# Start addresses of tiles in SBUF: three pads that move the operands of split matmuls to a multiple of 256 bytes

## The chip, the cores and the metric

The kernel runs on one core of a Trainium2 chip. The metric is the device time of one execution in microseconds (us), as the median of the runs. A core has TensorE (PE; its weight loads are listed as PEld), VectorE (DVE), ScalarE (ACT), GpSimd (POOL) and SyncE (SP, whose queue issues most of the DMAs), the memory SBUF with 128 partitions, and the accumulator PSUM.

## What is computed

A sequence of 512 tokens of width 1024 in float32 goes through two blocks of depth 2. Cut to what matters:

```python
# first block, for l in range(2)
mod = silu(c) @ w_ada[l] + b_ada[l]                      # 9 sections of 1024
h = rms_norm(x) * (1 + sc1) + sh1
x = x + 0.5 * g1 * (silu(h @ w_gate) * (h @ w_up)) @ w_ff1_out[l]     # 1024 -> 2816 -> 1024
h = rms_norm(x) * (1 + sc2) + sh2
z = h @ w_in[l]
x = x + g2 * concat(rwkv7(z_a), latent_attention(z_b), retention(z_c)) @ w_out[l]
h = rms_norm(x) * (1 + sc3) + sh3
x = x + 0.5 * g3 * (silu(h @ w_gate) * (h @ w_up)) @ w_ff2_out[l]
# second block, for l in range(2)
u = rms_norm(h) * norm1_g[l]
h = h + concat(pool(u), diff_attention(u), gated_linear_attention(u)) @ w_out_2[l]
h = h + relu(rms_norm(h) @ w_mlp1[l]) ** 2 @ w_mlp2[l]                # 1024 -> 4096 -> 1024
```

## The kernel before

Everything is kept with the features on the partitions and the 512 tokens along a row of 2048 bytes. A float32 product is made of three matmuls: each operand is split into a high and a low part of the type float32r, and `gemm_k` (line 405) issues high x high, high x low and low x high into one PSUM tile. `weight` (line 381) loads a block of weights, up to 1024 columns, into a `raw` tile by one DMA of the SP queue, ScalarE copies its 512-column halves into the high tile and VectorE subtracts to get the low tile; both are `wr` tiles. The activations are split in the same way by `split` (line 440) and `modulate`, into tiles of the classes `r` and `h`.

In a matmul's name in the profile, `ps<-a,b`, `a` is the operand that streams through (moving) and `b` the one that is loaded as weights (stationary). All large products are of this kind: `ps<-ff_h,wr` (feed-forward, in), `ps<-ff_r,wr` (feed-forward, out), `ps<-mix_h_x,wr`, `ps<-mix_r,wr`, `ps<-wr,mix_r` (the mixers' projections; the last has the weights moving), `ps<-mix_r_x,wr` and `ps<-mix_r_y,wr` (out of the first mixer), `ps<-mlp_r,wr` (both MLP products). Other matmuls of the mixers are plain float32; each of these shows as two records.

The program runs through the phases feed-forward, mixer 1, feed-forward, twice, then mixer 2, MLP, twice. The order of the instructions is fixed when the program is built. A dry pass notes the first and the last use of each tile, and `Alloc.assign` (line 175) gives each one of the fixed buffers of its class, by program order alone; sizes of tiles play no part in it. Each instruction is issued by `Spy` at line 136, so the profile shows L136 for all.

Where a tile lies follows from the order in which pools are opened and from the tiles' sizes, each rounded up to 32 bytes. `setup` (line 338) opens the constants: `ident`, `vec`, `masks`, `rows`, `ones`, then `x` (8 tiles of 2048 bytes), `mods`, `ident_r`. Then come the classes of `GLOBAL` (line 210) in their order: `raw`, `wr`, `m`, `mr`, `sq` (`ps` is PSUM). Behind them each phase opens its own classes (`KIND`, line 219; `PHASES`), and mixer 1 has places that pass from one class to another (`STAGES`, line 227): `va`, `big`, `s`, `r`, `h`. In the program of the kernel before, the first constant starts at byte 16,512 of a partition. The start of each tile, as its remainder by 256 bytes (its residue):

| tiles | start of the first, bytes | residue |
|---|---|---|
| `x` | 20,480 | 0 |
| `ident_r` | 37,824 | 192 |
| `raw` | 38,336 | 192 |
| `wr` | 50,624 | 192 |
| `m` | 75,200 | 192 |
| `mr` | 78,784 | 192, 224, 0, 32 |
| `sq` | 78,912 | 64 |
| all 512-column tiles of the phases (`s`, `r`, `h`) and `big`, `rw` | 80,960 | 64 |
| the same in the third stage of mixer 1 behind `va` (`mix_s_w`, `mix_r_y`, `mix_r_x`) | 193,728 for the last `mix_r_y` | 192 |

A slice of 128 columns of a weight tile starts at a multiple of 512 bytes from the tile's start, and half the tokens at 1024 bytes, so a slice has its tile's residue. The top of the allocation is at byte 228,544.

Of the kernel before, what the change touches and what calls it, by code (L numbers as in the profile page):

```python
# [12 lines left out]
F32 = mybir.dt.float32  # L13
F32R = mybir.dt.float32r
# [4 lines left out]
PSUM = bass.MemoryType.PSUM  # L19

P = 128
# [26 lines left out]
# ---------------------------------------------------------------- host layout  # L48
def blocks(w, cols=P):
    """[K, N] -> [N/cols, 128, K/128*cols]: one contiguous run per partition and block."""  # L50
    k, n = w.shape
    return np.ascontiguousarray(
        w.reshape(k // P, P, n // cols, cols).transpose(2, 1, 0, 3)
    ).reshape(n // cols, P, (k // P) * cols)


def group_blocks(w, groups):
    """[K, N] -> per group of K chunks: [N/128, 128, kg*128], flattened and joined."""
    return np.concatenate([blocks(w[a * P:(a + n) * P]).ravel() for a, n in groups])
# [11 lines left out]
OUT2_ROWS = np.r_[0:256, 768:1024, 256:768]  # L71
TWO_PI = (6.28125, 0.0019350051879882812, 3.019916e-07)


def make_masks():
    """constants that depend on shapes alone."""
# [23 lines left out]
def make_rows():  # L100
    """rotary frequencies and the sign of the sine, per partition, for head widths 64 and 32."""
    out = np.zeros((P, 4), np.float32)
    base = np.float32(10000.0)
    for j, d in ((0, 64), (2, 32)):
        inv = base ** (-np.arange(0, d, 2, dtype=np.float32) / np.float32(d))
        out[:, j] = np.tile(inv, P // (d // 2))
        out[:, j + 1] = np.where(np.arange(P) % d < d // 2, -1.0, 1.0)
    return out
# [11 lines left out]
# ---------------------------------------------------------------- device side  # L120
# [4 lines left out]
class Spy:  # L125
    """an engine that notes which tiles each instruction names, then issues it."""
# [21 lines left out]
class Alloc:  # L148
    """Tiles by class. A dry pass notes where each is used first and last in program order; from that each gets
    one of the class's fixed buffers, so that the buffers never force an order that the program doesn't have."""  # L150
# [17 lines left out]
    def begin(self, cls, key, n):  # L168
        """buffers (key, 0..n-1) that serve the class until `end`."""
# [5 lines left out]
    def assign(self, sizes):  # L175
        """key of the buffer for every tile, in the order of their birth."""
# [6 lines left out]
    def assign_with(self, sizes, keep):  # L183
        """the same, with `keep` buffers of a class held back from what fits into one that comes and goes."""
# [25 lines left out]
# class of buffer -> (shape, type, count); the phase's own classes follow  # L210
# [4 lines left out]
    "mr": ([P, 8], F32R, 4),  # L215
# [3 lines left out]
KIND = {"s": ([P, S], F32), "r": ([P, S], F32R), "h": ([P, S], F32R), "big": ([P, 1024], F32), "rw": ([P, 2048], F32), "va": ([P, 516], F32)}  # L219
# [6 lines left out]
# places of the first mixer that change their use: the stages' classes; "x" lies where "h" of the phase "ff" does  # L226
# [7 lines left out]
class Build:  # L234
# [36 lines left out]
    def stage(self, i):  # L271
        """the places from the first that changes on pass over to the classes of stage i."""
# [31 lines left out]
    def lend_x(self):  # L304
        """put x into DRAM; until it is back its tiles serve as the phase's slots."""
# [32 lines left out]
    def setup(self):  # L338
        nc, c = self.nc, self.const
        self.ident = c.tile([P, P], F32, name="ident")  # L340
# [14 lines left out]
    def background(self, share=None):  # L355
        """part of the work that goes on behind the first block's wide products (share None: all that is left)."""
# [23 lines left out]
    # -- weights: one block, split exactly into two float32r parts  # L380
    def weight(self, ap, n, cls="wr", sub=None):
        """(hi, lo) tiles of 512 columns each."""
# [17 lines left out]
    def gemm(self, out, w, x, ks, m=P, at=0, sl=ALL):  # L400
        """out[m, 512] = sum_k w_k^T x_k, each product of split parts; w's chunks from column `at` on."""
# [3 lines left out]
    def gemm_k(self, out, w, xk, i, n, m=P, at=0, sl=ALL):  # L405
        """chunk i of n of such a product."""
# [7 lines left out]
    def out_proj(self, load, g, update, norm=None, scale=None):  # L414
        """x[j] from its products with g, for all j. norm "sum": with the sums of squares of the next norm, the last
        j's left to `pending`; "halves": with the norm itself, the last two j by halves of the tokens, so that the first half's is there early."""
# [33 lines left out]
    # -- rsqrt of a small positive tile by DVE  # L450
# [14 lines left out]
    def sum_sq(self, acc, xc, sl=ALL):  # L465
        """acc + xc^2 (acc None: a new sum)."""
# [10 lines left out]
    def x_done(self, j, sl=ALL):  # L477
        """chunk j of x has its final value of this stage: its part of the next norm."""
        self.xsq = self.sum_sq(None if j == 0 else self.xsq, self.x[j], sl)

    def norm_half(self, i):
        """PSUM [128, 512], half i of the tokens: one over the norm of x."""
# [3 lines left out]
    def rms_col(self, chunks, dim, eps, ts=range(4)):  # L486
        """[128, 4]: 1/sqrt(mean over features of x^2 + eps) of token ts[t]*128 + partition; chunks None: of x."""
# [15 lines left out]
    def bcast(self, r, ts=range(4)):  # L503
        """PSUM [128, 512] with the token's value on every partition."""
# [9 lines left out]
    # -- adaptive layer norm: one section of 1024 columns  # L514
    def cond_row(self):
        """silu(c) on every partition."""
# [13 lines left out]
    def ada_dot(self, l, s, k, w):  # L530
        """chunk k of section s of 1024 columns of the modulation of layer l, less its bias."""
# [3 lines left out]
    def ada_end(self, l, s, k=0, n=KD):  # L535
        """chunks k.. of section s with their bias, and what is derived from them."""
# [10 lines left out]
    def ada_steps(self, parts):  # L547
        """the sections (layer, section) one after the other in small steps, loads ahead of them."""
# [13 lines left out]
    def modulate(self, i, k, hk, pr, sl=ALL, pool=True):  # L562
        """chunk k of h = rms_norm(x) * (1 + sc) + sh, split into hk."""
# [13 lines left out]
    def modulated(self, i, ws):  # L577
        """h of modulation i, a list of (hi, lo), and its products with the first weights, by halves of the tokens
        and as the chunks come."""
# [11 lines left out]
    def start(self):  # L591
        """the first h: its modulation is worked out chunk by chunk as the weights for it come in."""
# [26 lines left out]
    def ff(self, l, w, i, norm):  # L619
        """x += 0.5 * g * (silu(h w_gate) * (h w_up)) w_out"""  # L620
# [32 lines left out]
    # ------------------------------------------------------------ constants  # L653
    def restart(self):
        """factors of a scan over the tokens that starts anew with every chunk of 64."""
# [9 lines left out]
    def rotary_tables(self):  # L665
        """cos and signed sin of positions * inv, [128, 512] each, for head widths 64 and 32."""
# [26 lines left out]
    def derived(self, l):  # L693
        """small per-feature vectors worked out on chip for layer l of the first block."""
# [14 lines left out]
    # ------------------------------------------------------------ first mixer: RWKV-7  # L709
# [11 lines left out]
    def rwkv_z(self, l, h, ps, dv, z):  # L721
        """nine projected tiles after the centred shift (r 0-1, k 2-3, v 4-5, gate, decay and rate inputs);
        v with the chunks of each pair swapped."""
# [16 lines left out]
    def head_bcast(self, col, stride, at):  # L740
        """PSUM [128, 512] from token-major scalars of two heads, col[tok, t*stride + at + hh]."""
# [10 lines left out]
    def head_sums(self, src, dst, at):  # L752
        """dst[tok, t*2 + at + hh] = sum over the head's 64 features of src [features, tok]."""
# [4 lines left out]
    def rwkv_norm(self, l, z, j):  # L758
        """one over the norm of each head's keys, token major."""
# [19 lines left out]
    def rwkv_prep(self, l, z, dv, lora, j):  # L779
        """the four scaled operands of each direction for one pair of heads.  # L780

        pr: [d, step pair, (p | r), (par, t)]; qm: [d, step pair, par, (q | m swapped by par), t]
        """
# [57 lines left out]
    def rwkv_inverse(self, os_):  # L841
        """X^T of every chunk, X = (1 + strict part)^-1: per pair of heads and direction
        [128 (par, s)][(step pair, hh), t]."""
# [29 lines left out]
        # matrix (j, m, d, (par, half)) on its own partition, m = (step pair, hh)  # L873
# [37 lines left out]
    def rwkv_blocks(self, xt, xa, u):  # L911
        """from the inverses of the 32 x 32 diagonal blocks those of the chunks, for one pair of heads."""
        nc = self.nc
        # off-diagonal 32-blocks
# [34 lines left out]
    def rwkv_pair(self, o, vs, xt, xd, ip):  # L949
        """per-chunk matrices of one pair of chunks in each direction: what the sequential steps need.  # L950
        xd: zeros, and room for the inverses of both chunks on the diagonal."""
# [88 lines left out]
    def rwkv_heads(self, l, z, o, xt, gate, j, out):  # L1040
        """one pair of heads: sequential steps over the chunks, head norm, bonus, gate."""
# [5 lines left out]
        # the state by turns in two halves, both heads' [key, value] on the diagonal for each direction  # L1047
# [32 lines left out]
        # head norm (the values were centred, so the mean is zero), gain, bonus, gate  # L1080
# [54 lines left out]
    # ------------------------------------------------------------ first mixer: latent attention  # L1135
# [19 lines left out]
    def rope32(self, out, pz, n, tab):  # L1155
        """rotary over 32-wide heads on n partitions; pz in PSUM."""
# [8 lines left out]
    def mla_norms(self, l, z):  # L1165
        """the two latent norms, in place."""
# [8 lines left out]
    def mla_first(self, z, i, pk, pq, kq, qpe):  # L1175
        """operands of head i: [64 plain, 32 rotary, 1 for the maximum] x tokens, split."""
# [9 lines left out]
        # the maximum of a row of scores, taken of the rounded operands: any number near it serves  # L1186
        mx, mr = self.small_t(4, "mla_max"), self.get("mr")
# [10 lines left out]
    def mla_second(self, i, kq, va, ot):  # L1198
        """softmax and values of head i, keys on partitions; ot[tok, (tile, hh, v)]."""
# [29 lines left out]
    def mla_pair(self, ot):  # L1229
        """the values of a pair of heads, features on partitions, split."""  # L1230
# [12 lines left out]
    def mla(self, l, z, out, others):  # L1243
# [4 lines left out]
        # rotary part of the queries, four heads a tile  # L1248
# [9 lines left out]
        # values, token major, a column of ones between the two heads of a pair  # L1258
# [728 lines left out]
```

## Time and profile before

| | |
|---|---|
| time, median of 3 runs | 3662.97 us (3648.62, 3662.97, 3664.79) |
| span of the profiled execution (its own time isn't listed apart) | 3653.2 us |
| TensorE busy | 3528.1 us (97%), 17786 matmuls |
| VectorE busy | 2103.8 us (58%) |
| ScalarE busy | 1436.7 us (39%) |
| GpSimd busy | 281.7 us (8%) |
| DMA moved | 375.78 MB, 103 GB/s on average |

The span is the time from the first to the last instruction of one profiled execution; the device time has a little more around it. Busy times overlap between engines. Matmuls are pipelined: the end of one is modelled, the next starts before it, and so a mean duration of 395 ns doesn't say how far apart two matmuls are. How far apart they are is read from the start times in the timeline. [...] Residues stand in no view; they come from the table above.

### The profile page before, as it was taken

The numbers are of one execution on the slowest core, as the hardware profiler recorded it, in microseconds if no ns is written. First come the engines' busy times: TensorE is split into PE (matmuls) and PEld (weight loads), VectorE is DVE, ScalarE is ACT, GpSimd is POOL, SyncE is SP. The second block draws the span as 40 slices with busy tenths as digits, with TensorE's granted clock in tenths as the row PEclk, the third lists the DMA queues.
The fourth block names the chain that finished last, engine by engine and source line by source line (L and its number), as shares of the span: only waits on it lengthen the run. The fifth ranks groups of instructions, "written<-read, shape, count | busy, mean of one in ns | idle before, by whom it ended". The sixth has DMA issues, their size and how long they took to land. (4 is left out here: it accounts for less than half of the span.)

```text
span 3653.2 us, 46456 instructions
## 1 busy us (share of the span) xinstructions
PE 3528.1 (97%) x17786; PEld 2849.3 (78%) x17786; DVE 2103.8 (58%) x4153; ACT 1436.7 (39%) x2644; POOL 281.7 (8%) x344
## 2 busy tenths in 40 slices
PE   7999998999999999999899999999999999999998
PEld 5888876788888888887678888877778887778887
DVE  7954785657954534468565544366754445764444
ACT  3223544444233423245344423245443334443333
POOL 2000261100000000015210000000100000000000
PEclk9999998999999999999898999999999999999999
DMA  7833322015842222332201222221122222212222
GB/s 273 323 123 103 120 81 54 24 46 207 322 164 95 86 97 87 96 121 81 61 18 41 76 93 94 96 83 64 54 94 93 97 94 72 65 58 98 93 93 75
DMA packets 132879, 375.78 MB, mean 103 GB/s; under 512 B 37712, under 2 KB 41072, under 8 KB 132656
## 3 DMA queue, kind: packets, MB, share of 16 engines
q1 hardware_dynamic: 127808, 359.48, 29.7%
q0 software_dynamic: 3776, 12.32, 1.0%
q8 instruction: 139, 2.28, 0.3%
q10 hardware_dynamic: 1072, 1.01, 0.1%
q14 instruction: 84, 0.69, 0.1%
HBM read 362.27 MB, written 10.49 MB: 102 GB/s over the span
## 5 line engine op out<-in xcount | busy, mean ns | idle before, releaser
L136 ACT CAST wr<-raw 128x512 fp32r<-128x512 f32 (+2 forms) x1054 | 640.8, 610 | 1558.7 <-PE ps L136 1438.5
L136 DVE TENSOR_TENSOR wr<-raw,wr 128x512 fp32r<-128x512 f32 (+1 forms) x1004 | 681.4, 680 | 782.3 <-ACT wr L136 760.6
L136 PE MATMUL ps<-ff_h,wr 128*128 128x512 f32 (+1 forms) x4296 | 983.7, 390 | 10.1 <-ACT ff_h L136 7.3
L136 PEld LDWEIGHTS ps<-ff_h,wr 128*128 128x128 f32 x4296 | 794.4, 190 | 195.4 <-ACT ff_h L136 10.1
L136 PE MATMUL ps<-mlp_r,wr 128*128 128x512 f32 (+1 forms) x3120 | 716.3, 391 | 2.1 <-ACT mlp_r L136 2.1
L136 PEld LDWEIGHTS ps<-mlp_r,wr 128*128 128x128 f32 x3120 | 580.9, 188 | 135.7 <-ACT mlp_r L136 3.0
L136 PE MATMUL ps<-ff_r,wr 128*128 128x512 f32 (+1 forms) x2238 | 495.2, 382 | 0.0
L136 PEld LDWEIGHTS ps<-ff_r,wr 128*128 128x128 f32 x2238 | 404.1, 188 | 89.3
L136 PE MATMUL ps<-mix_r,wr 128*128 128x512 f32 (+1 forms) x1104 | 277.9, 402 | 1.8 <-DVE mix_s L136 1.8
L136 PE MATMUL ps<-mix_h_x,wr 128*128 128x512 f32 (+2 forms) x1104 | 261.0, 395 | 4.3 <-ACT mix_h_x L136 2.2
L136 PEld LDWEIGHTS ps<-mix_r,wr 128*128 128x128 f32 (+1 forms) x1104 | 199.4, 185 | 57.9 <-issue 5.2
L136 PEld LDWEIGHTS ps<-mix_h_x,wr 128*128 128x128 f32 (+1 forms) x1104 | 200.4, 197 | 56.0 <-issue 4.5
L136 DVE SCALAR_TENSOR_TENSOR ff_big<-ff_big,ff_big 128x1024 f32<-128x1024 f32 x144 | 176.5, 1238 | 10.3 <-DMA ff_big<-in_w_ada 9.6
L136 DVE SCALAR_TENSOR_TENSOR ff_s<-ff_s,ps 128x512 f32<-128x512 f32 x176 | 120.2, 684 | 88.1 <-PE ps L136 83.7
L136 DVE SCALAR_TENSOR_TENSOR x<-ps,hg,x 128x512 f32<-128x512 f32 (+1 forms) x102 | 73.4, 719 | 85.9 <-PE ps L136 85.7
L136 DVE TENSOR_TENSOR ps<-ps,mlp_s 128x512 f32<-128x512 f32 (+1 forms) x66 | 45.1, 683 | 105.3 <-PE ps L136 105.2
L136 ACT COPY mix_s<-ps 128x256 f32<-128x256 f32 (+7 forms) x156 | 61.6, 401 | 104.4 <-PE ps L136 75.8
L136 DVE TENSOR_TENSOR mlp_r<-mlp_s,mlp_r 128x512 fp32r<-128x512 f32 x80 | 54.6, 691 | 69.5 <-ACT mlp_r L136 69.5
L136 POOL MEMSET mix_s<- 32x256 f32 (+3 forms) x36 | 12.5, 348 | 985.6 <-DVE mix_r L136 363.9
L136 ACT ACTIVATE mix_s<-ps,m 128x512 f32<-128x512 f32 (+3 forms) x140 | 70.9, 529 | 44.0 <-PE ps L136 25.0
L136 PE MATMUL ps<-mix_s,mix_s 128*128 128x128 f32 (+7 forms) x648 | 82.7, 283 | 2.6 <-ACT mix_s L136 1.9
L136 PEld LDWEIGHTS ps<-mix_s,mix_s 128*128 128x128 f32 (+5 forms) x648 | 63.6, 169 | 16.9 <-ACT mix_s L136 7.1
(317 smaller groups left out, 3591.8 us busy)
## 6 DMA issues: line engine op xcount, KB each, us to landing
raw<-in_ff_in SPq DMA_DIRECT2D x176, 512.0 KB, 3.5
ff_big<-in_w_ada SPq DMA_DIRECT2D x144, 512.0 KB, 6.2
raw<-in_mlp SPq DMA_DIRECT2D x128, 512.0 KB, 3.5
raw<-in_ff_out SPq DMA_DIRECT2D x64, 448.0 KB, 3.3
raw<-in_ff_out SPq DMA_DIRECT2D x32, 512.0 KB, 3.6
raw<-in_out SPq DMA_DIRECT2D x32, 512.0 KB, 3.5
raw<-in_in SPq DMA_DIRECT2D x28, 512.0 KB, 3.5
raw<-in_in_a SPq DMA_DIRECT2D x18, 512.0 KB, 4.0
```

The lines of the kernel that those rows point to most:

```text
L136: self.alloc.last[self.name] = f(*a, **k)
```

## The change

Three pads and nothing else that reaches the program (comments and docstrings are taken out too): one constant tile of 16 floats (64 bytes) ahead of all others; `mr` gets 32 columns instead of 8 (128 bytes instead of 32, four tiles); `va` gets 528 columns instead of 516 (2112 bytes instead of 2080 after rounding, four tiles). The two uses of the padded tiles take a slice of the old width. By adding up, `raw`, `wr`, `m`, `mr`, `sq`, `ident_r` and all tiles of the phases then start at residue 0 (`va` at 0, 64, 128 and 192), `x` at 64, and the top of the allocation is at byte 229,120.

```diff
+LINE = 256
+ALIGN_PAD = 16
...
-    "mr": ([P, 8], F32R, 4),
+    "mr": ([P, 32], F32R, 4),
...
-KIND = {"s": ([P, S], F32), "r": ([P, S], F32R), "h": ([P, S], F32R), "big": ([P, 1024], F32), "rw": ([P, 2048], F32), "va": ([P, 516], F32)}
+KIND = {"s": ([P, S], F32), "r": ([P, S], F32R), "h": ([P, S], F32R), "big": ([P, 1024], F32), "rw": ([P, 2048], F32), "va": ([P, 528], F32)}
...
     def setup(self):
         nc, c = self.nc, self.const
+
+        c.tile([P, ALIGN_PAD], F32, name="align_pad")
         self.ident = c.tile([P, P], F32, name="ident")
...
-        mx, mr = self.small_t(4, "mla_max"), self.get("mr")
+        mx, mr = self.small_t(4, "mla_max"), self.get("mr")[:, :8]
...
             v = self.get("va")
-            v3 = v.rearrange("p (n b) -> p n b", n=4)
+            v3 = v[:, :516].rearrange("p (n b) -> p n b", n=4)
```

## Rows read from the trace of the kernel before

**Rows 1.** Page, busy time, share of the span and instructions of each engine:
```profile
PE 3528.1 (97%) x17786; PEld 2849.3 (78%) x17786; DVE 2103.8 (58%) x4153; ACT 1436.7 (39%) x2644; POOL 281.7 (8%) x344
```

**Rows 2.** TensorE's waits: for whom, us in total, times, longest; first and last of 16:
```profile
PE ps L136 <- DVE sq L136: 27.1, 7, 17.2
...
PE ps L136 <- POOL ff_h L136: 0.4, 2, 0.2
```

**Rows 3.** Stretches: us, busy of PE, PEld, DVE, ACT, POOL; clock, DMA share, GB/s:
```profile
90.00:120.00 30.00, 30.00 (x130) 24.31 (x129) 29.76 (x55) 9.28 (x16) 0.00 (x0) 1.00 0.93 328
2740.00:2923.00 183.00, 183.00 (x789) 148.39 (x788) 77.10 (x116) 69.00 (x114) 0.00 (x0) 1.00 0.29 95
```

**Rows 4.** Groups of TensorE by shape, whole span: count, busy us, mean ns, idle before:
```profile
L136 PE MATMUL ps<-ff_h,wr 128*128 128x512 f32 x4008 | 942.2, 396 | 5.9 <-ACT ff_h L136 5.5 <-DVE ff_h L136 0.3
L136 PE MATMUL ps<-mlp_r,wr 128*128 128x512 f32 x3024 | 704.3, 395 | 2.1 <-ACT mlp_r L136 2.1
L136 PE MATMUL ps<-ff_r,wr 128*128 128x512 f32 x1986 | 464.4, 395 | 0.0
L136 PE MATMUL ps<-mix_r,wr 128*128 128x512 f32 x1056 | 265.8, 403 | 0.0
L136 PE MATMUL ps<-mix_h_x,wr 128*128 128x512 f32 x864 | 220.8, 413 | 1.7 <-DVE mix_s L136 1.7
...
L136 PE MATMUL ps<-wr,mix_r 128*128 128x512 f32 x192 | 46.2, 398 | 2.9 <-ACT mix_r L136 2.9
```

**Rows 5.** Timeline of TensorE, dense stretches: start us, length us, run, count:
```profile
2699.74 60.58 PE L136 MATMUL ps<-mlp_r,wr 128*128 128x512 f32 x260
...
2200.86 59.43 PE L136 MATMUL ps<-ff_h,wr 128*128 128x512 f32 x254
```

**Rows 6.** Timeline of TensorE, end of mixer 1, first and last of five blocks:
```profile
2021.27 2.20 PE L136 MATMUL ps<-mix_r_y,wr 128*128 128x512 f32 x9
...
2043.03 2.20 PE L136 MATMUL ps<-mix_r_y,wr 128*128 128x512 f32 x9
```

**Rows 7.** Timeline of TensorE, first feed-forward stage, weights in `ff_r` tiles:
```profile
63.57 1.98 PE L136 MATMUL ps<-ff_h,ff_r 128*128 128x512 f32 x8
```

**Rows 8.** Timeline of TensorE, two runs of 24 with `wr` moving:
```profile
2446.09 5.83 PE L136 MATMUL ps<-wr,mix_r 128*128 128x512 f32 x24
...
1880.67 5.71 PE L136 MATMUL ps<-wr,mix_r_x 128*128 128x512 f32 x24
```

**Rows 9.** By tile, durations min/median/max ns: 2700 to 2760 us, 2021 to 2047 us:
```profile
L136 PE MATMUL ps<-mlp_r,wr x260: 390/393/404, 2699.7 to 2759.9; 128*128 128x512 f32 x130
...
L136 PE MATMUL ps<-mix_r_x,wr x71: 389/389/389, 2020.8 to 2046.9; 128*128 128x512 f32 x71
```

**Rows 10.** Timeline of 256-column runs; below, plain float32 groups (count, busy, mean ns):
```profile
526.83 9.40 PE L136 MATMUL ps<-wr,mix_h_x 128*128 128x256 f32 x77 [0.68 <-DVE wr L136]
...
2049.22 1.96 PE L136 MATMUL ps<-mix_r_x,wr 128*128 128x256 f32 x15
...
L136 PE MATMUL ps<-x,x 64*128 64x512 f32 x32 | 15.8, 615 | 0.0
L136 PE MATMUL ps<-mix_s_x,mix_s 128*64 128x512 f32 x28 | 10.8, 618 | 0.0
```

**Rows 11.** Groups of TensorE by shape, first 183 us:
```profile
L136 PE MATMUL ps<-ff_h,wr 128*128 128x512 f32 x369 | 92.3, 408 | 5.6 <-ACT ff_h L136 5.2 <-DVE ff_h L136 0.3
L136 PE MATMUL ps<-ff_r,wr 128*128 128x512 f32 x192 | 44.8, 394 | 0.0
```

**Rows 12.** Groups of VectorE by shape, whole span, the subtraction that makes a low part:
```profile
L136 DVE TENSOR_TENSOR wr<-raw,wr 128x512 fp32r<-128x512 f32 x926 | 641.7, 694 | 728.9 <-ACT wr L136 720.3 <-PE ps L136 6.8
L136 DVE TENSOR_TENSOR mlp_r<-mlp_s,mlp_r 128x512 fp32r<-128x512 f32 x80 | 54.6, 691 | 69.5 <-ACT mlp_r L136 69.5
```

## The prediction

> **What bounds the kernel now.** I read the page's busy times first: TensorE is busy in 3528.1 us, 97% of the span [rows 1]. The list of TensorE's waits comes next: its longest entry, over the whole span, is 27.1 us and its last 0.4 [rows 2], so there is little waiting to remove. [...] So the question is the step from one matmul's start to the next one's, and whether it depends on where the operands lie.
>
> The busy column can't answer that (matmuls overlap); the timeline can, because a run of n equal matmuls lasts n-1 steps plus the duration of the last. In the dense runs of the change's main operands, 260 matmuls take 60.58 us and 254 take 59.43 us [rows 5]; less a last duration of 0.39 us these are 60.19 / 259 = 232.4 ns and 59.04 / 253 = 233.4 ns a step. In both, the moving operand (`mlp_r`, `ff_h`) starts at residue 64 of 256 bytes and the stationary one (`wr`) at residue 192.
>
> The kernel before also holds pairs at *equal* residues, and these are my experiment. In the last projection of the first mixer, both `mix_r_x`/`mix_r_y` and `wr` are at 192. There the blocks of nine that begin at 2021.27 and 2043.03 us [rows 6] are 4 x 24 matmuls apart: 21.76 us / 96 = 226.67 ns. All durations in that stretch are 389 ns, where the dense MLP run spreads over 390 to 404 with a median of 393 [rows 9]; the modelled duration moves one for one with the step. A second pair has both operands at 64: eight matmuls of `ff_h` with `ff_r` in 1.98 us [rows 7], (1.98 - 0.39) / 7 = 227 ns. The control is moving `wr` (192): with stationary `mix_r` at 64, 24 matmuls take 5.83 us; with stationary `mix_r_x` at 192, 5.71 us [rows 8]. Both runs follow small matmuls and contain their own start, so their means, 5.44 / 23 = 236.5 and 5.32 / 23 = 231.3 ns, stand a little above the settled steps; the difference is 5.2 ns a step. So neither 64 nor 192 is bad in itself: unlike residues cost about 6 ns a matmul, in either direction.
>
> **What the change does, part by part.** No instruction is added or removed and no order changes; the dry pass sees the same uses, so each tile gets the same buffer number. Only addresses move. I add them up from the sizes: the 64-byte pad takes `raw`, `wr` and `m` from residue 192 to 0; the wider `mr` (4 x 96 bytes more) takes the phase pools `s`, `r`, `h`, `big`, `rw` from 64 to 0; the wider `va` (4 x 32 bytes more) takes the third-stage pools `mix_r_y`, `mix_r_x` from 192 to 0. The top of the allocation goes from 228,544 to 229,120 bytes of a partition. After it, moving and stationary operands of the split products start at the same residue, 0; `x` goes the other way, from 0 to 64.
>
> *Large matmuls.* The 512-column products with unlike residues are six groups: 4008 + 1986 + 3024 + 1056 + 864 + 192 = 11,130 [rows 4]. I take the step to fall to 226.67 ns wherever TensorE is the bound.
> - Feed-forward stages: 4008 + 1986 less the 369 + 192 of the first 183 us [rows 11] leave 5433. The measured steps of such stretches lie between 232.4 and 233.4, so 5.7 to 6.7 ns, mean 6.2: 33.7 us.
> - MLP stages: 3024 x 5.7 ns = 17.2 us.
> - Mixer stages: 1056 + 864 + 192 = 2112, x 5.8 ns = 12.2 us if all were dense; mean durations of 403 and 413 against 395 [rows 4] show waits among them, and a wait swallows the gain before it. I keep three quarters, 9.2 us; the ends are 5 and 12.
> - First 183 us: 561 x 5.8 = 3.2 us at most. But VectorE is busy 29.76 of 30 us there, at a DMA share of 0.93 [rows 3], so a faster TensorE meets the modulation's dot products. I keep 0.5; the ends are 0 and 3.2.
> - Start after a wait: the like run of rows 8 is 5.32 - 23 x 0.2267 = 0.11 us above the settled step, the unlike one 5.44 - 23 x 0.2324 = 0.09. So a start costs the like pairs some 0.02 us more; the list of waits has 16 entries with 73 waits [rows 2], 1.5 us. I take off 2.
>
> The sum is 33.7 + 17.2 + 9.2 + 0.5 - 2 = 58.6 us.
>
> *Half-width matmuls* (256 columns): a run at 192/64 has 77 in 9.40 us, 9.12 / 76 = 120.0 ns; one at 192/192 has 15 in 1.96 us, 1.68 / 14 = 120.0 ns [rows 10]. I count 0.
>
> *Plain float32 matmuls* (not split): 512 columns with both operands at 0 take 615 ns, with both at 64 618 ns [rows 10]. No trend that I could use, so 0; the bound is 3 ns on some 4080 records, 12 us either way, and most of these stand beside waits of the mixers.
>
> *VectorE, ScalarE, DMA.* The same subtraction takes 694 ns on tiles at 192 and 691 on tiles at 64 [rows 12]: 0, and it is hidden in dense stretches anyway (77 of 183 us busy). If that cover went, 3 ns on 926 subtractions would be 2.8 us. The weight transfers are at 0.29 of the DMA engines there [rows 3]; a TensorE that is 2.5% faster asks for 0.30. No wait changes and nothing is queued behind anything new.
>
> [...] Rows 8 show the step of one moving operand change with the place of the stationary one alone. [...]
>
> **The rivals.**
> 1. *Nothing moves* (3663 us). The like pairs of the kernel before might be fast for something else that they share, such as the stretch they stand in, or residue 0 might not behave like 64 and 192. For: no split product in the trace has both operands at 0, and the longest like stretch (rows 6) is some 30 us. Against: two places, three operand pairs, and the control in both directions. This is also "the change doesn't do what it says". Chance 0.11.
> 2. *It settles on the slow step* (slower). Moving and stationary operands, and the tiles being written, now all start at residue 0; if two streams that start alike at 0 got into each other's way at every matmul, each one would pay what only some pay now. The place is the dense stretch and the price is the slowest matmul of it: 404 ns, 15 above 389 [rows 9], so a step of 226.7 + 15 = 241.7 instead of 232.9 (the mean of the two runs of rows 5), 8.8 ns x 11,130 = 98 us: 3761 us. It decides the sign as soon as the mean step at 0/0 is above 232.9 ns. Against it: the like pairs at 64 and at 192 do the opposite. Chance 0.04.
> 3. *The fast step doesn't hold*: with raw tiles, weights and every pool at one residue, writes of ScalarE, VectorE and the DMAs start where the reads do and throw TensorE out of the fast step again and again. Half of the gain: 3663 - 29 = 3634 us. Against: in the stretch of rows 6 VectorE and ScalarE write `wr` at 192 as well, and all durations stay at 389. Chance 0.06.
> 4. *More than that*: residue 0 is better still. [...] Nothing in the trace points to it. Chance 0.03.
>
> **How the numbers follow.** The forecast has 0.76. The profiled execution has a span of 3653.2 us; its own time isn't listed beside the three runs (3648.62 to 3664.79, median 3662.97), so I take the 9.8 us between span and median as what lies around it and leave it alone. The span becomes 3653.2 - 58.6 = 3594.6 us, the median 3604 us (-1.6%). Its own bounds: at best 36.4 (5433 x 6.7 ns) + 17.2 + 12.2 + 3.2 = 69 us, from the lowest of the runs 3580; at worst 31.0 (5433 x 5.7 ns) + 17.2 + 5 - 2, less the 12 us of the float32 matmuls, 39 us, from the highest run 3626. To hold 8 in 10 the range reaches on to rival 3: 3580 to 3640. About 0.5% (18 us) is what a measurement of this kernel can tell from no change. Faster by more than that: forecast, rivals 3 and 4, 0.85; within it: rival 1, 0.11; slower: rival 2, 0.04.
>
> **What would show it.** In the profile after, a dense run of `mlp_r` with `wr` must have a step of 226.67 ns, so 260 matmuls in 59.1 us instead of 60.58, with a median duration of 389. The three feed-forward groups must fall alike, the 256-column runs and the subtractions must not move. If dense durations stay at 393, rival 1 holds; at 400 or more, rival 2; if they jump between 389 and 393 or more within a run, rival 3. The forecast is wrong by size if the steps are right but the mixers or the first 183 us give back more than the 6 us I left out: then TensorE's waits grow by that amount.

## The result, and the profile after

The changed kernel takes 3600.8 us (median of four runs, 3596.28 to 3616.28), the kernel before, beside it on the same chip, 3658.47 us (four runs, 3648.62 to 3664.79). The ratio is 0.9854 with a 95% interval of 0.9826 to 0.9881: 57.7 us less, faster by three times the 0.5% that a measurement of this kernel can tell. The forecast was 3604 us and 58.6 us less.

The page of the kernel after, its span and its busy times (us, share, instructions):

```profile
span 3614.5 us, 46456 instructions
PE 3487.3 (96%) x17786; PEld 2858.0 (79%) x17786; DVE 2100.4 (58%) x4153; ACT 1437.4 (40%) x2644; POOL 281.3 (8%) x344
```

The work is the same, instruction for instruction, and only TensorE's time is less [rows 1]. This profiled execution is the slowest of the four, 3616.28 us; a later run of the same kernel has a span of 3597.9 us. Why its span fell by only 38.7 us is told below, with the first mixer.

The groups by shape answer [rows 4] (count, busy us, mean ns, idle before):

```profile
L138 PE MATMUL ps<-ff_h,wr 128*128 128x512 f32 x4008 | 918.0, 390 | 5.7 <-ACT ff_h L138 5.3 <-DVE ff_h L138 0.3
L138 PE MATMUL ps<-mlp_r,wr 128*128 128x512 f32 x3024 | 687.4, 389 | 2.1 <-ACT mlp_r L138 2.1
L138 PE MATMUL ps<-ff_r,wr 128*128 128x512 f32 x1986 | 452.1, 389 | 0.0
L138 PE MATMUL ps<-mix_r,wr 128*128 128x512 f32 x1056 | 261.4, 399 | 0.0
L138 PE MATMUL ps<-mix_h_x,wr 128*128 128x512 f32 x864 | 215.5, 407 | 2.1 <-DVE mix_s L138 2.1
L138 PE MATMUL ps<-wr,mix_r 128*128 128x512 f32 x192 | 46.9, 403 | 2.9 <-ACT mix_r L138 2.9
```

Line 138 here is line 136 of before. Read the busy column against [rows 4]: -24.2, -16.9, -12.3, -4.4, -5.3, +0.7, together -62.4 us over 11,130 matmuls. The mean of the MLP group is now the smallest duration, 389: nearly all of its matmuls run at the same pace.

The timeline of dense stretches (start us, length us, run, count) answers [rows 5]:

```profile
2199.70 60.68 PE L138 MATMUL ps<-ff_h,wr 128*128 128x512 f32 x267
2699.74 60.46 PE L138 MATMUL ps<-mlp_r,wr 128*128 128x512 f32 x266
```

(60.46 - 0.39) / 265 = 226.7 ns, and (60.68 - 0.39) / 266 = 226.7 ns, where [rows 5] gave 232.4 and 233.4. Durations by tile, minimum, median and maximum in ns, from 2700 to 2760 us, to be read against the first line of [rows 9]:

```profile
L138 PE MATMUL ps<-mlp_r,wr x266: 389/389/389, 2699.7 to 2759.8; 128*128 128x512 f32 x133
```

The stretches answer [rows 3] (us, busy of PE, PEld, DVE, ACT, POOL, granted clock, DMA share, GB/s):

```profile
90.00:120.00 30.00, 30.00 (x134) 24.86 (x133) 30.00 (x55) 10.21 (x17) 0.00 (x0) 1.00 0.91 338
2740.00:2923.00 183.00, 183.00 (x809) 151.56 (x808) 78.96 (x119) 69.78 (x116) 0.64 (x2) 1.00 0.28 96
```

In the dense stretch 809 matmuls start where 789 did, 2.5% more, at the same granted clock of 1.00: the gain is not a higher clock.

From the first matmul of a phase to the first of the next (the last MLP to the end of the span), in us, read from the timelines of four profiled executions:

| | feed-forward, four stages | MLP, two | second mixer, two | first mixer, two |
|---|---|---|---|---|
| before | 1514.9 | 736.0 | 479.9 | 895.6 |
| before, once more | 1516.5 | 737.3 | 482.7 | 882.2 |
| after | 1478.4 | 719.2 | 477.7 | 912.2 |
| after, once more | 1478.4 | 719.2 | 474.6 | 899.0 |

As an example, the lines between which the first MLP lies, of the kernel before (361.06 us):

```profile
2676.74 8.20 PE L136 MATMUL ps<-mlp_r,wr 128*128 128x512 f32 x34 [1.04 <-ACT mlp_r L136]
...
3037.80 8.41 PE L136 MATMUL ps<-wr,mix_r 128*128 128x512 f32 x35 [1.88 <-ACT mix_r L136]
```

and of the kernel after (352.56 us):

```profile
2656.81 8.11 PE L138 MATMUL ps<-mlp_r,wr 128*128 128x512 f32 x34 [1.06 <-ACT mlp_r L138]
...
3009.37 9.84 PE L138 MATMUL ps<-wr,mix_r 128*128 128x512 f32 x35 [1.88 <-ACT mix_r L138]
```

The feed-forward stages give 36.5 us, the MLP stages 16.8, the second mixer 2.2 to 5.3 (first row against the last two). The first mixer gives nothing that can be seen: its length varies by more than its gain from one execution of the same program to the next.

### The profile page after: what moved, and what is told of

Read it like the earlier page. It is cut to its first block, busy times and chain, and to the rows that moved or that the text cites. A ratio compares the mean times of both kernels' runs of the same rounds, so it can differ in the third digit from the quotient of the medians.

```text
span 3614.5 us, 46456 instructions
## 1 busy us (share of the span) xinstructions
PE 3487.3 (96%) x17786; PEld 2858.0 (79%) x17786; DVE 2100.4 (58%) x4153; ACT 1437.4 (40%) x2644; POOL 281.3 (8%) x344
## 5 line engine op out<-in xcount | busy, mean ns | idle before, releaser
L138 PE MATMUL ps<-ff_h,wr 128*128 128x512 f32 (+1 forms) x4296 | 960.7, 385 | 9.5 <-ACT ff_h L138 7.1
L138 PE MATMUL ps<-mlp_r,wr 128*128 128x512 f32 (+1 forms) x3120 | 699.4, 386 | 2.1 <-ACT mlp_r L138 2.1
L138 PE MATMUL ps<-ff_r,wr 128*128 128x512 f32 (+1 forms) x2238 | 483.0, 377 | 0.0
L138 PE MATMUL ps<-ident,mix_s 128*128 128x128 f32 x384 | 59.4, 299 | 20.5 <-DVE mix_s L138 20.2
```

Of the source, the lines that this page charges most:

```text
L138: self.alloc.last[self.name] = f(*a, **k)
```

## The experiments

The theory: what sets the step of a 512-column split matmul is whether its moving and its stationary operand start at the *same* residue by 256 bytes; the value of the residue does not matter, nor does the place of `raw`. The rivals: it is the multiple of 256 itself that is fast, for the moving operand, for the weights, or for the raw tiles that ScalarE and VectorE read; or only some distances between the operands are slow. Later, three forms of the theory had to be told apart. Where an expectation speaks of 1a, 1b and 1c: in 1a the matmul pays whose own operands are unlike, in 1b the one that runs while unlike weights are loaded, and in 1c an unlike operand takes the fast step away from a whole stretch.

All edits are to the changed kernel. A pad class takes room in a partition and is used by nothing. Ratios go by the runs of the kernel before on the same chip.

| run | residue of weights / moving | time, us (n: one run) | ratio, 95% interval | step, dense stages, ns |
|---|---|---|---|---|
| `like_at_64` | 64 / 64 | 3593.72 | 0.9848 [0.9795, 0.9901] | 226.7 |
| `like_at_32` | 32 / 32 | 3594.71 | 0.9855 [0.981, 0.9901] | 226.7 |
| `first_pad_alone` | 0 / 128 | 3662.48 | 1.0016 [0.9984, 1.0047] | 232.9, 233.3 |
| `apart_by_phase` | 0 / 32 to 224 | 3661.37 (n) | | 228.9 to 234.3 |
| `after_beside` | 0 / 0 | 3603.92 | 0.9866 [0.9826, 0.9905] | 226.7 |
| `raw_apart` | 0 / 0, `raw` at 128 | 3603.79 | 0.9852 [0.982, 0.9883] | 226.7 |
| `low_weights_apart` | high parts 0, low parts 128 / 0 | 3645.72 (n) | | 231.1 |
| `odd_tiles_apart` | 0 / 0 and 128 by turns, first MLP | 3627.36 (n) | | 232.5 there |
| `third_stage_apart` | 0 / 128 in one stage | 3618.12 (n) | | 232.4 there |

**Like residues elsewhere (`like_at_64`, `like_at_32`).** The first pad is 128 (or 96) bytes instead of 64. `mr` goes back to its old width, and a pad of 128 bytes behind it keeps the phases at the residue of the weights.

```diff
-ALIGN_PAD = 16
+ALIGN_PAD = 32
...
-    "mr": ([P, 32], F32R, 4),
+    "mr": ([P, 8], F32R, 4),
+    "pad_b": ([P, 32], F32, 1),
```

For `like_at_32` the first constant is 24.

> Weights, raw tiles and the phases' pools all start at residue 64 of 256 bytes instead of 0 (the pad ahead of the constants is 128 bytes, 128 bytes stand behind mr). Theory 1, equal residues: as fast as the changed kernel, ratio to before 0.985, dense step 226.67 ns, all durations 389. Theory 2, the multiple of 256 itself: as before, ratio 1.00, step 232 to 233 ns, durations 390 to 404.

> The same with residue 32, so that no operand starts at a multiple of 64 bytes. Theory 1, equal residues: ratio 0.985, step 226.67 ns. Theory 2, the multiple itself (256, 128 or 64): ratio 1.00 or above, step 232 ns or more.

Durations by tile from 2700 to 2760 us, of the kernel at 64:

```profile
L138 PE MATMUL ps<-mlp_r,wr x267: 389/389/390, 2699.7 to 2759.9; 128*128 128x512 f32 x134
```

and of the kernel at 32:

```profile
L138 PE MATMUL ps<-mlp_r,wr x267: 389/389/390, 2699.6 to 2759.9; 128*128 128x512 f32 x134
```

Neither kernel has a weight tile or a 512-column tile at a multiple of 256, and both have the whole gain, with ratios that can't be told from that of the change. The multiple of 256 that the change aims at is not what works; that the operands are alike is. Nor is it the remainder by 512: in the kernel at 64, by adding up, `wr` starts at byte 50,752 (64 more than a multiple of 512) and the first `r` tile of the MLP at 105,792 (320 more), and the gain is whole. By its ratio no kernel tried here beats the changed one; these two equal it.

**The first pad alone (`first_pad_alone`).** `mr` and `va` go back to their old widths. `raw` and `wr` stay at 0, the phases go to 128.

```diff
-    "mr": ([P, 32], F32R, 4),
+    "mr": ([P, 8], F32R, 4),
...
-KIND = {"s": ([P, S], F32), "r": ([P, S], F32R), "h": ([P, S], F32R), "big": ([P, 1024], F32), "rw": ([P, 2048], F32), "va": ([P, 528], F32)}
+KIND = {"s": ([P, S], F32), "r": ([P, S], F32R), "h": ([P, S], F32R), "big": ([P, 1024], F32), "rw": ([P, 2048], F32), "va": ([P, 516], F32)}
```

> Only the first of the three pads: raw and weight tiles at residue 0, the pools at 128, so unlike by 128 as in the kernel before (64 and 192) but with the weights at a multiple of 256. Theory 1, equal residues: no gain, ratio 1.00, step 232 to 233 ns. Theory 2 in the form that the weights' place alone counts: ratio 0.985, step 226.67 ns.

```profile
L138 PE MATMUL ps<-mlp_r,wr x258: 392/396/398, 2719.8 to 2779.8; 128*128 128x512 f32 x129
...
L138 PE MATMUL ps<-mix_r_x,wr x67: 389/389/390, 2023.7 to 2046.8; 128*128 128x512 f32 x67
```

Aligned weights and raw tiles alone are worth nothing: 1.0016. In the same kernel the last stage of the first mixer, where moving tiles happen to lie at 0 like the weights, runs at 389. So the fast and the slow step stand side by side in one execution, and the place tells them apart.

**All distances (`apart_by_phase`).** A class opened first in six of the phases moves their tiles by 32 to 224 bytes; the weights stay at 0.

```diff
+APART = {0: 96, 2: 32, 3: 64, 5: 160, 7: 192, 9: 224}
...
+            apart = APART.get(self.nphase, 0)
...
-            classes = {c: (*KIND[c], n) for c, n in PHASES[name].items()}
+            classes = {"gap": ([P, apart // 4], F32, 1)} if apart else {}
+            classes.update({c: (*KIND[c], n) for c, n in PHASES[name].items()})
```

> Weights at 0 and each phase's pools at a distance of its own: feed-forward stages 96, 32, 64 and 160 bytes, MLPs 192 and 224, mixers 0. One look at the steps of each phase. Theory 1, equal residues: every phase but the mixers is back at 232 to 233 ns, some 15 us a feed-forward stage counting 1500 matmuls at 6 ns is 9 us, all six 54 us, so about 3655 us. A finer rule (distances that are multiples of 64 are alike, say): 64 and 192 stay at 226.67 ns and 32, 96, 160, 224 don't.

(The expectation's 15 us for a stage is a slip: 1500 matmuls at 6 ns are 9 us.) The timeline, one run from each stage, in the order 96, 32, 64, 160, 192, 224:

```profile
248.98 39.36 PE L138 MATMUL ps<-ff_r,wr 128*128 128x512 f32 x168
...
1004.73 55.46 PE L138 MATMUL ps<-ff_h,wr 128*128 128x512 f32 x237
...
1299.75 36.32 PE L138 MATMUL ps<-ff_h,wr 128*128 128x512 f32 x158
...
2208.79 51.47 PE L138 MATMUL ps<-ff_h,wr 128*128 128x512 f32 x219
...
2719.62 60.59 PE L138 MATMUL ps<-mlp_r,wr 128*128 128x512 f32 x259
...
3329.73 60.60 PE L138 MATMUL ps<-mlp_r,wr 128*128 128x512 f32 x259
```

Length less 0.39, by the count less one: 233.3, 233.3, 228.9, 234.3, 233.3 and 233.4 ns. With the 232.4 to 233.4 at a distance of 128, six of the seven unlike distances cost the same 6 to 8 ns. The seventh, the moving tile 64 bytes on from the weights, costs 2.2; 64 bytes the other way (192) costs the full price. So it is not a matter of distance alone, and no run shows why 64 stands out.

**The raw tiles (`raw_apart`).** Weights and phases at 0 as in the change; `raw` goes to 128 and `x` to 192.

```diff
-ALIGN_PAD = 16
+ALIGN_PAD = 48
...
+    "pad_c": ([P, 32], F32, 1),
...
-    "mr": ([P, 32], F32R, 4),
+    "mr": ([P, 8], F32R, 4),
+    "pad_b": ([P, 32], F32, 1),
```

`pad_c` stands between `raw` and `wr`.

> Weights and pools at residue 0 as in the changed kernel, but the raw tiles at 128 and x at 192. Theory 1, only the two operands of a matmul count: ratio 0.985, dense step 226.67 ns, the subtraction into wr near 694 ns, the weight transfers near 3.5 us to landing. Theory 2, the place of the raw form has a part in the gain (the DMA that writes it, or the copy that reads it): ratio between 0.985 and 1.00, transfers or copies longer.

> The changed kernel once more, beside the next three on one chip: ratio 0.985 to before, dense step 226.67 ns.

The groups of VectorE and ScalarE that read `raw`, of this kernel:

```profile
L138 DVE TENSOR_TENSOR wr<-raw,wr 128x512 fp32r<-128x512 f32 x926 | 641.2, 694 | 700.1 <-ACT wr L138 691.8 <-PE ps L138 7.0
...
L138 ACT CAST wr<-raw 128x512 fp32r<-128x512 f32 x976 | 604.1, 620 | 1403.2 <-PE ps L138 1288.4 <-issue 102.8 <-DVE ff_big L138 4.2
```

and of the changed kernel:

```profile
L138 DVE TENSOR_TENSOR wr<-raw,wr 128x512 fp32r<-128x512 f32 x926 | 640.9, 693 | 694.7 <-ACT wr L138 686.3 <-PE ps L138 7.1
...
L138 ACT CAST wr<-raw 128x512 fp32r<-128x512 f32 x976 | 605.1, 621 | 1397.8 <-PE ps L138 1285.3 <-issue 102.7 <-DMA raw<-in_ff_in 2.6
```

694 and 693 ns, 620 and 621; the time is 3603.79 us beside 3603.92 of the changed kernel in the same series. Where `raw` lies has no part in the gain, so aligning the raw tiles does nothing for the time.

**One operand of three unlike (`low_weights_apart`).** Of each three products of a split pair two use the high part of the weights and one the low part. The low parts get a class of their own, 128 bytes off.

```diff
-    "wr": ([P, 512], F32R, 12),
+    "wr": ([P, 512], F32R, 6),
+    "pad_c": ([P, 32], F32, 1),
+    "wl": ([P, 512], F32R, 6),
...
-    "mr": ([P, 32], F32R, 4),
+    "mr": ([P, 24], F32R, 4),
...
-            hi, lo = self.get(cls), self.get(cls)
+            hi, lo = self.get(cls), self.get("wl" if cls == "wr" else cls)
```

> Low parts of the weights (now named wl) at 128, high parts (wr) and all pools at 0. One matmul in three has an unlike pair, and its weights are loaded while the matmul ahead of it streams. Theory 1a, a matmul's own two operands must agree all the time: the mean step rises by a third of 6 ns, to about 228.7 ns, and the matmuls with wl are the long ones. Theory 1b, what counts is the moving operand that streams while the next weights are loaded: the same mean, but the matmuls ahead of wl (with wr) are the long ones. Theory 1c, the fast step needs an unbroken run of like pairs: the mean is back at 232 ns or more and all durations spread.

The timeline of a dense stretch of the first MLP, first and last of five triples, then the durations:

```profile
2740.06 0.40 PE L138 MATMUL ps<-mlp_r,wl 128*128 128x512 f32 x1
2740.30 0.62 PE L138 MATMUL ps<-mlp_r,wr 128*128 128x512 f32 x2
2740.75 0.40 PE L138 MATMUL ps<-mlp_r,wl 128*128 128x512 f32 x1
...
2743.53 0.40 PE L138 MATMUL ps<-mlp_r,wl 128*128 128x512 f32 x1
```

```profile
L138 PE MATMUL ps<-mlp_r,wr x174: 389/392/396, 2719.7 to 2779.8; 128*128 128x512 f32 x174
...
L138 PE MATMUL ps<-mlp_r,wl x87: 397/397/397, 2720.0 to 2779.6; 128*128 128x512 f32 x87
```

Fifteen matmuls take 2743.53 - 2740.06 = 3.47 us, 231.3 ns each; over all dense stretches the mean is 231.1. Sorted by place in the triple, the start times of the first MLP give 232.5 ns for the `wr` matmul ahead of `wl` (during which the unlike weights are loaded: in the timeline of the kernel after, the load of an `ff_r` weight starts at 63.42 us and its matmul at 63.64, while the run of six matmuls ahead goes from 62.26 to 63.80), 234.1 for `wl` itself and 226.67 for the one behind. So one unlike operand of three costs (5.8 + 7.4) = 13 ns on two steps, and the third is untouched. That is neither 1a nor 1b alone, both of which come to 228.7, but the two together, and not 1c, since the third step stays fast. When everything is unlike, the two costs do not add up to 13 on each step; it stays at 6 (232.4 ns in the kernel before).

**Moving operands by turns (`odd_tiles_apart`).** In the first MLP every other tile of class `r` starts at 128; the second MLP is left as it is.

```diff
+ROW_PAD = {7: 32, 9: 0}
...
+            if name == "mlp":
+                classes["r"] = ([P, S + ROW_PAD[self.nphase - 1]], F32R, PHASES[name]["r"])
...
-        return self.get("r") if dt == F32R else self.get("s", dt)
+        return self.get("r")[:, :S] if dt == F32R else self.get("s", dt)
```

> In the first MLP alone the tiles that hold the activations are 128 bytes wider, so that every other one starts at 128 instead of 0 (616 of its 1536 matmuls have an unlike moving operand); all else as in the changed kernel. Theories 1a and 1b: the mean step of this MLP is about 226.7 + 0.4 x 6 = 229 ns, between 226.7 and 232.4, the second MLP stays at 226.7. Theory 1c: 232 ns or more in the first MLP. Span about 3597 to 3605 us.

The timeline, a run of the first and one of the second MLP:

```profile
2719.75 60.59 PE L138 MATMUL ps<-mlp_r,wr 128*128 128x512 f32 x259
...
3299.80 60.46 PE L138 MATMUL ps<-mlp_r,wr 128*128 128x512 f32 x266
```

60.20 / 258 = 233.3 ns in the first, 60.07 / 265 = 226.7 in the second. The first MLP lasts 361.2 us, as long as before (361.1 and 362.5), with only about two of five moving operands unlike: I had expected 229 ns a step. By place (the start times, sorted by the tile that each matmul reads, where the neighbours are alike), the step of a matmul on an unlike tile is 233.6 ns, the one ahead of it 235.9, the one behind 230.0. An unlike moving operand thus reaches both neighbours, and a stage with two in five of them gains nothing. Its total of 3627.36 us is one run (a span of 3625.6 us, where 3597 to 3605 was expected), and holds a first mixer of 915.7 us besides; the stage is what counts here.

**The third pad (`third_stage_apart`).** The first two shifts as in the change, `va` at its old width: only the third stage of the first mixer is unlike.

```diff
-    "mr": ([P, 32], F32R, 4),
+    "mr": ([P, 8], F32R, 4),
+    "pad_b": ([P, 96], F32, 1),
...
-KIND = {"s": ([P, S], F32), "r": ([P, S], F32R), "h": ([P, S], F32R), "big": ([P, 1024], F32), "rw": ([P, 2048], F32), "va": ([P, 528], F32)}
+KIND = {"s": ([P, S], F32), "r": ([P, S], F32R), "h": ([P, S], F32R), "big": ([P, 1024], F32), "rw": ([P, 2048], F32), "va": ([P, 516], F32)}
```

> The first two pads without the third: weights and pools at 0, but the third stage of the first mixer at 128 from the weights. By what the runs so far show, the last projection of that mixer (steps of mix_r_x and mix_r_y with wr) goes from 226.67 to about 233 ns, some 550 matmuls x 6 ns = 3 us over both depths, below what a time can show; all other dense steps stay at 226.67 ns. If the third pad had no part, these steps stay at 226.67 ns too.

The timeline of the last projection of the first mixer, two blocks of nine that are 2 x 24 matmuls apart:

```profile
815.28 2.25 PE L138 MATMUL ps<-mix_r_y,wr 128*128 128x512 f32 x9
...
826.44 2.25 PE L138 MATMUL ps<-mix_r_y,wr 128*128 128x512 f32 x9
```

11.16 us / 48 = 232.5 ns, where [rows 6] had 226.67. In the kernel before, this stage was alike by accident (192 and 192); moving `wr` and the phases breaks it, and the third pad puts it back. Taken alone that pad brings nothing new: by an estimate (492 matmuls x 5.8 ns) it keeps some 3 us from being lost, which no single time can show.

**The first mixer's length (`before_again`).** The kernel before, one more execution.

> The kernel before once more, for how much its first mixer differs from one execution to the next with nothing changed. If the mixer's length goes with the granted clock there and not with the change: some 10 us up or down against the first profile, with dense stages that agree within 0.3 us. If the change lengthens the mixer: the same 445 and 450 us as in the first profile.

Its first mixer takes 439.5 and 442.7 us, against 445.1 and 450.4 in the profile before (some 10 us of difference were expected); the feed-forward and MLP stages repeat within 1.4 us each, where 0.3 was expected. The boundaries in the timeline of the kernel after (first matmul of the mixer, first of the next phase):

```profile
401.39 0.50 PE L138 MATMUL ps<-mix_h_x,wr 128*128 128x256 f32 x2 [1.11 <-ACT mix_h_x L138]
...
858.48 0.50 PE L138 MATMUL ps<-ff_h,wr 128*128 128x256 f32 x2 [0.33 <-ACT ff_h L138]
```

and of `after_beside`, the same program:

```profile
844.84 0.51 PE L138 MATMUL ps<-ff_h,wr 128*128 128x256 f32 x2 [0.33 <-ACT ff_h L138]
```

which begins the mixer at 401.11. So the same program needs 457.1 us in one execution and 443.7 in the next. The stretches show what differs (columns as above); of the kernel after:

```profile
401.39:858.48 457.09, 426.81 (x2826) 347.05 (x2826) 290.40 (x627) 209.46 (x413) 102.26 (x124) 0.91 0.18 55
```

of `after_beside`:

```profile
401.11:844.84 443.73, 413.29 (x2826) 335.93 (x2826) 290.25 (x627) 209.36 (x413) 102.04 (x124) 0.94 0.18 57
```

and of the two executions of the kernel before, first

```profile
409.55:854.69 445.14, 415.35 (x2827) 337.54 (x2827) 289.89 (x627) 209.32 (x413) 102.61 (x124) 0.94 0.19 56
```

then `before_again`:

```profile
409.37:848.87 439.50, 410.24 (x2827) 331.46 (x2827) 289.92 (x627) 209.21 (x413) 103.06 (x124) 0.96 0.19 57
```

The other engines' busy times agree to half a microsecond; PE's go with the granted clock, 0.96, 0.94, 0.94, 0.91. At the same 0.94 the changed kernel is 1.4 us shorter, less than a hundredth of the clock is worth (0.94 against 0.96 is 5.6 us). Over twelve profiled executions both depths of this mixer take 885.8 to 915.7 us in the eight where its operands are alike (the one with an unlike third stage among them), and 882.2 to 901.8 in the four where many of them are not: no gain to be seen, and none that could be, at such a spread. Whether a denser TensorE is itself what lowers the clock there can't be told from these runs.

Sorted by where the mixer's own tiles start, the same twelve do differ: the seven with these tiles at residue 0, the changed kernel's place, take 899.0 to 915.7 us (mean 907.6), the five with them at 32, 64 or 128 take 882.2 to 901.8 (mean 890.7). So residue 0 may cost the first mixer some 17 us; `like_at_64` and `like_at_32` have the gain without it (888.2 and 885.8 us). No experiment was made for this and the twelve ran on several chips, so neither the effect nor a cause is shown.

## Why the prediction was right

- *The step.* Predicted 226.67 ns for like operands; measured 226.7 in the dense stages, 389 for nearly every duration. The thesis (equality, not the multiple) was read from three pairs of operands of the kernel before [rows 6 to 8], and holds for 0, 32 and 64.
- *Feed-forward.* Predicted 33.7 and 0.5 for the first 183 us, 34.2 us; the two groups fell by 36.5 and the stages by 36.5.
- *The first 183 us* is a mis-sized term: predicted 0.5 us, since VectorE was busy 29.76 of 30 us [rows 3] and would be late next. The groups of this stretch in the kernel after, against [rows 11]:

```profile
L138 PE MATMUL ps<-ff_h,wr 128*128 128x512 f32 x381 | 93.4, 403 | 5.4 <-ACT ff_h L138 5.1 <-DVE ff_h L138 0.3
```

  Twelve matmuls more (381 against 369) fit into it, 12 x 226.7 ns = 2.7 us, close to the upper end of 3.2. VectorE is now busy 30.00 of 30 us between 90 and 120, and TensorE starts 134 matmuls there instead of 130: the full VectorE did not bound TensorE here, which in these 183 us waits for it three times (17.4, 3.5 and 0.3 us), as often and as long as in the kernel before.
- *MLP.* Predicted 17.2; the group fell by 16.9, the stages by 16.8.
- *Mixers.* Predicted 9.2; the three groups fell by 4.4 + 5.3 - 0.7 = 9.0 us of busy time. On the path 2.2 to 5.3 us of it are seen in the second mixer; the rest is lost in the swings of the first. Of the 57.7 us between the medians the 36.5 and 16.8 of the other stages leave 4.4 for all mixers, so this term was sized at about twice what came of it. TensorE's whole busy time fell by only 40.8 us, not 62.4: in the two depths of the first mixer it rose from 837.4 to 852.1 us, at a granted clock of 0.91 and 0.92 instead of 0.94 and 0.93. One plain float32 group took 618 ns [rows 10] and 685 in the two executions of the kernel before, 886 and 819 in those of the kernel after. The two executions of the kernel before have the same addresses and differ by the clock: from 610 to 616 us it is 1.00 in the first, and twelve records of the group take 2.17 us,

```profile
610.86 2.17 PE L136 MATMUL ps<-mix_s_x,mix_s 128*64 128x512 f32 x12
```

  and 0.65 in `before_again`, where they take 3.64:

```profile
611.03 3.64 PE L136 MATMUL ps<-mix_s_x,mix_s 128*64 128x512 f32 x12
```

  So the duration of this group can't be read without the clock. Another group, on `x`, whose place did change (0 to 64), stayed at 615. Of the kernel after:

```profile
L138 PE MATMUL ps<-x,x 64*128 64x512 f32 x32 | 15.8, 615 | 0.0
...
L138 PE MATMUL ps<-mix_s_x,mix_s 128*64 128x512 f32 x28 | 14.3, 886 | 0.0
```

- *Nothing for the 256-column runs, float32, VectorE, ScalarE and the DMAs.* The eight largest groups of 256 columns went from 190.7 to 192.2 us, +1.5 and no gain (1.3 of it in `ff_h`, 42.7 to 44.0, which takes 43.8 in `before_again` too); the subtraction takes 693 ns, 694 before [rows 12]; 512 KB transfers into `raw` land after 3.4 to 3.8 us by group, 3.5 to 4.0 before. Right, to within what two executions of one program differ by.
- *Waits after the faster steps.* Predicted -2 us for starts and no growth of waits. TensorE's list of waits (us, times, longest) has, of after:

```profile
PE ps L138 <- DVE mix_s L138: 28.5, 14, 6.8
PE ps L138 <- DVE sq L138: 27.3, 7, 17.4
```

  The second was 27.1 [rows 2], the first 25.2: 3.3 and 0.2 us more. All entries of the list together went from 116.8 to 119.0 us: what the faster steps give is hardly given back in waits. Whether a start after a wait costs like pairs 0.02 us more, as the forecast has it, no run shows apart from this.
- *What lies around the span.* The text took the 9.8 us between span and median for it. This was wrong: 3616.28 - 3614.5 = 1.8 us lies around the span, and the rest was the spread of the runs. The difference does not hang on it.
- *The rivals.* Nothing moves, a slow step at 0/0 and a better one at 0 all fell with the step of 226.7 ns, and half the gain with the durations of 389/389/389. The fastest settled step of any run here is 226.67 ns, and no run shows a better one at 0. Nor is the place of the weights indifferent to the 512-column matmuls: in `low_weights_apart` only the low weights were moved (and the twelve buffers made two sets of six), and it cost 13 ns in every three matmuls.
- *The sum.* 58.6 us forecast and 57.7 measured lie closer than the parts do: the feed-forward came out 2.3 us above its terms, the mixers some 5 below theirs, and the 2 us taken off for starts were not seen as such. The interval of the ratio is 44 to 64 us. The step and the two large terms were right; that the sum is right to 0.9 us is luck.

*Why* operands that start alike are faster was not shown: the runs show where the cost falls (5.8 and 7.4 ns in `low_weights_apart`), not what makes it.

## What to carry to other kernels

When TensorE is busy without a gap, read the step from the start times of a long run, not the mean duration, and compare it between places where the same shape has other operands: the kernel before held both the slow and the fast pair (232.4 and 226.67 ns), and one subtraction showed the 2.5%. In a kernel of 512-column float32r products, add up where tiles start and let every moving and every stationary operand of them start at the same remainder by 256 bytes: 0, 32, 64 and 192 all gave 226.7 ns here. Do it for all of them, since a stage with two unlike moving operands in five had no gain left (361.2 us beside 361.1 and 362.5). Before crediting a few microseconds to a change, look at how far a stage repeats in two executions of one program: the feed-forward and MLP stages here did to 1.4 us, the first mixer to 13 us a depth.

## What the runs showed of the hardware

- The step of a 512-column float32r matmul with its own weight load (granted clock 1.00 in the dense stretches of the kernels before and after): 226.7 ns when both operands start at the same residue by 256 bytes (0, 32, 64 and 192 seen), 232.4 to 234.3 at six unlike distances (32, 96, 128, 160, 192 and 224 bytes), 228.9 when the moving tile starts 64 bytes on from the weights. The exception is unexplained. Remainders by 512 need not agree (64 and 320 in `like_at_64`, 226.7 ns).
- The price is not one matmul's own. One unlike weight tile among three costs 5.8 ns on the matmul during which it is loaded and 7.4 on its own (`low_weights_apart`); an unlike moving tile between like ones costs 9.2 ns on the matmul ahead of it, 6.9 on its own and 3.3 on the one behind (`odd_tiles_apart`). With all operands unlike by 128 bytes, the price is some 6 ns a matmul throughout (232.4 to 233.4 ns a step).
- 256-column matmuls (120.0 ns a step [rows 10]), VectorE's subtraction (693 and 694 ns), ScalarE's cast (620 and 621 ns) and the 512 KB transfers into `raw` (3.4 to 4.0 us) showed no such effect.
- The first mixer, a stage of many small matmuls and waits, took 457.1 and 443.7 us in two executions of one program, at a granted clock of 0.91 and 0.94.
